# Sums of w_down: smaller transfers spread over the up stage, and half of the sums read back through the weights' buffers

## The chip, the core and the metric

The kernel runs on one core of a Trainium2 chip. The metric is the device time of one execution in microseconds, as the median of three runs. TensorE multiplies, ScalarE (ACT) and VectorE (DVE) prepare its operands, SyncE (SP) issues nearly all loads, and GpSimd (POOL) issues a few stores.

## The reference

It is one block of a hybrid transformer layer in float32 on 256 rows of width 2048: three attention branches, a gated merge and a projection, and behind them a gated feed-forward part. Only the latter bears on the change:

```
h2 = rms_norm(x, g_ffn)
u  = causal_depthwise_conv(h2 @ w_up, conv_w, conv_b)      # 2048 x 11264
u_gate, u_val = split(u, 2)
x  = x + (silu(u_gate) * u_val) @ w_down                   # 5632 x 2048
```

## The kernel before, in words

Every float32 weight is split into a high part (a rounded copy, made by ScalarE) and a low part (the rest, made by VectorE), and a product is formed from two or three matmuls with these parts. A weight tile therefore passes through four hands: a load into a buffer `raw`, a copy to `hi`, a subtraction to `lo`, and the matmuls. The pool `wp` has four buffers of each kind, of 4 KB in each of 128 partitions. A `raw` buffer is free for the next load when its low part is done; a `hi` or `lo` buffer is free when its last matmul has read it. SyncE works through its loads in one order, and each waits for its buffer, so a load that waits holds all that stand behind it.

The **up stage** (line 775 on) walks over w_up in 22 groups, one for each four feature tiles f0 and each half s of the columns (s = 0 the gate, s = 1 the value). A group has eight rounds over k. Each round loads one tile of 512 KB (line 142), splits it (143, 144) and issues 16 matmuls (791, 792). When a group is over, `conv` is queued for its two pairs of tiles, and its instructions (lines 726 to 748) run on ScalarE and VectorE beside the next group. After the value half, conv also multiplies gate and value and stores the result as `aT` (745 to 748), so the groups with s = 0 carry the longer conv.

The **down stage** uses one level of Strassen's scheme for a part of its work. An "eight" multiplies two tiles of k in the plain way: 8 products, 24 matmuls of 512 columns. A "seven" multiplies two tiles of k with 7 products, 21 matmuls; for it sums of w_down's blocks and sums of the activations are needed. The sums of the activations (`forms`, lines 818 to 836, result `sf`) are made by VectorE and ScalarE during the down stage. The sums of w_down are made already in the up stage by `weight_sums` (line 755): in each of the first 18 groups it loads two rows of tiles, 1 MB, into `r` (line 760), makes four additions on VectorE (764 to 768) and stores 1 MB to a tensor T in DRAM from GpSimd's queue (770). The pool `sp` holds two buffers `r`. In the down stage `seven` (line 884) loads two tiles of w_down, 256 KB and 512 KB, into `raw` buffers and the two halves of T, 512 KB each, called t13 and t42, into buffers `tt` of a pool `dn` (line 843). This pool has two buffers `tt` and lies on the memory of the convolution's pool, so it opens when the last convolution is over.

The two halves of the output's columns are done one after the other. The order of eights (e) and sevens (s) is written out in `PLANS` (line 40). A scheduler orders the instructions of each engine by what it takes to be ready, except for those that are kept in program order; the loads of `raw` tiles, the splits in the up stage and the additions on `r` keep to it as far as the code marks them. The stores to T are the only work of GpSimd's queue in this stage.

## Time and profile before

| what | value |
|---|---|
| median of three runs | 1524.01 us |
| the three runs | 1524.01, 1516.52, 1524.95 us |
| the profiled execution's own time | 1516.09 us |
| its span, first to last instruction | 1514.4 us |
| mean granted TensorE clock | 0.998 |
| up stage with sums | about 765 to 1180 us of the span |
| up stage without | 1180 to 1270 us |
| down stage | 1270 to 1508 us |
| TensorE busy | 1492.3 us, 99% of the span |

Times within the profile are microseconds from the span's start. In a timeline row stand the start, the duration, the engine, the line of the kernel, the operation with its output and inputs and, in brackets, how long the engine had stood idle and what ended that. Rows of waits give the engine and line that waited, what it waited for, the total, how often, and the longest. Rows of the chain of waits give start, duration and the work on the chain. Matmuls overlap each other in the trace, so the distance from one start to the next tells their pace, and not their duration.

### The profile page before, as it was taken

To read this page: it belongs to the slowest core of one execution; us is meant where nothing else is said; L and a number is where in the kernel's file an instruction comes from. 1 tells how busy PE (TensorE), PEld (TensorE's weight loads), DVE (VectorE), ACT (ScalarE), POOL (GpSimd) and SP (SyncE) were. 2 spreads that over 40 slices of the span, in tenths; PEclk is the share of its full clock that TensorE was granted. 3 is DMA by queue.
4 is the path that set the end of the run, shared out by engine and by line. 5 is a ranking of instruction groups with operands and counts; after the bars stand their busy time and mean duration, and the time that the engine had idled before them with its cause. 6 is when DMAs were issued, how large, how long until landed. Compare 5 with 4: busy or idle time off the path is not lost.

```text
span 1514.4 us, 20053 instructions
## 1 busy us (share of the span) xinstructions
PE 1492.3 (99%) x7411; PEld 1254.3 (83%) x7411; DVE 1021.5 (67%) x1291; ACT 856.8 (57%) x1211; POOL 25.8 (2%) x64
## 2 busy tenths in 40 slices
PE   9999999999999999999999999999999999899998
PEld 7888888888888888888888888888888888788876
DVE  5766566455655556565567778778778767877666
ACT  6755455368444444444566757657667766564553
POOL 0000000001000000000000000000000000000000
PEclk9999999999999999999999999999999999999999
DMA  8675475475666666665587787787877765787875
GB/s 299 202 205 155 130 219 154 127 215 154 194 200 208 191 205 194 192 193 184 182 264 267 248 296 255 271 282 257 294 279 249 223 196 171 263 280 258 262 271 176
DMA packets 151504, 335.55 MB, mean 222 GB/s; under 512 B 10714, under 2 KB 19566, under 8 KB 149102
## 3 DMA queue, kind: packets, MB, share of 16 engines
q1 hardware_dynamic: 147486, 313.29, 65.6%
q0 software_dynamic: 2592, 18.88, 3.0%
q10 hardware_dynamic: 1328, 2.11, 0.4%
q8 instruction: 58, 0.95, 0.3%
q14 instruction: 40, 0.33, 0.1%
HBM read 313.26 MB, written 20.97 MB: 221 GB/s over the span
## 4 chain that ended last, share of the span: by engine, by line
PE 74%; DMA 9%; DVE 9%; ACT 5%; issue 3%; POOL 0%; SPq 0%; DVEq 0%; ACTq 0%; POOLq 0%
PE u L791 9%; DMA raw_u<-in_w_up_dram 7%; PE g L154 5%; PE g L156 5%; PE g L155 5%; PE u L792 5%; PE d L859 4%; PE d L858 4%; PE d L857 4%; DVE lo_u L144 3%; PE s L154 2%; PE s L156 2%; PE f L154 2%; PE s L155 2%; PE f L155 2%
## 5 line engine op out<-in xcount | busy, mean ns | idle before, releaser
L791 PE MATMUL u<-hT,hi_u 128*128 128x512 f32 x1408 | 495.7, 397 | 0.1
L792 PE MATMUL u<-hT,lo_u 128*128 128x256 f32 x1408 | 396.0, 281 | 7.6 <-DVE lo_u L144 7.6
L791 PEld LDWEIGHTS u<-hT,hi_u 128*128 128x128 f32 x1408 | 264.3, 188 | 63.7 <-issue 0.5
L144 DVE TENSOR_TENSOR lo_u<-raw_u,hi_u 128x1024 fp32r<-128x1024 f32 x176 | 213.5, 1219 | 95.5 <-ACT hi_u L143 95.4
L792 PEld LDWEIGHTS u<-hT,lo_u 128*128 128x128 f32 x1408 | 265.9, 189 | 10.7 <-DVE lo_u L144 10.4
L143 ACT CAST hi_u<-raw_u 128x1024 fp32r<-128x1024 f32 x176 | 181.8, 1048 | 144.0 <-DMA raw_u<-in_w_up_dram 87.6
L144 DVE TENSOR_TENSOR lo_g<-raw_g,hi_g 128x1024 fp32r<-128x1024 f32 x96 | 117.6, 1228 | 101.4 <-ACT hi_g L143 98.8
L143 ACT CAST hi_g<-raw_g 128x1024 fp32r<-128x1024 f32 x96 | 100.8, 1052 | 121.7 <-PE g L155 97.5
L154 PE MATMUL g<-hi_g,xT 128*128 128x512 f32 x384 | 150.9, 393 | 0.0
L156 PE MATMUL g<-lo_g,xT 128*128 128x512 f32 x384 | 149.6, 390 | 0.0
L155 PE MATMUL g<-hi_g,xT 128*128 128x512 f32 x384 | 149.5, 389 | 0.0
L852 ACT CAST hi_d<-raw_d 128x1024 fp32r<-128x1024 f32 (+1 forms) x88 | 83.6, 963 | 42.5 <-PE d L858 29.6
L853 DVE TENSOR_TENSOR lo_d<-raw_d,hi_d 128x1024 fp32r<-128x1024 f32 (+1 forms) x88 | 95.1, 1110 | 15.0 <-ACT hi_d L852 15.0
L857 PE MATMUL d<-hi_d,aT 128*128 128x512 f32 x246 | 95.7, 389 | 0.0
L858 PE MATMUL d<-hi_d,aT 128*128 128x512 f32 x246 | 95.7, 389 | 0.0
L859 PE MATMUL d<-lo_d,aT 128*128 128x512 f32 x246 | 95.7, 389 | 0.0
L156 PEld LDWEIGHTS g<-lo_g,xT 128*128 128x128 f32 x384 | 72.1, 188 | 15.4
L155 PEld LDWEIGHTS g<-hi_g,xT 128*128 128x128 f32 x384 | 72.1, 188 | 14.5
L154 PEld LDWEIGHTS g<-hi_g,xT 128*128 128x128 f32 x384 | 72.1, 188 | 14.5
L738 ACT ACTIVATE z<-u,taps 128x256 f32<-128x256 f32 x176 | 74.6, 496 | 0.0
L739 DVE TENSOR_TENSOR y<-y,z 128x512 f32<-128x512 f32 x88 | 60.7, 690 | 19.1 <-ACT z L738 16.3
L853 DVE TENSOR_TENSOR lo_t<-tt,hi_t 128x1024 fp32r<-128x1024 f32 x36 | 44.1, 1225 | 39.8 <-ACT hi_t L852 39.7
(314 smaller groups left out, 2617.0 us busy)
## 6 DMA issues: line engine op xcount, KB each, us to landing
raw_u<-in_w_up_dram SPq DMA_DIRECT2D x176, 512.0 KB, 4.7
raw_g<-in_w_in_dram SPq DMA_DIRECT2D x96, 512.0 KB, 3.7
raw_d<-in_w_down_dram SPq DMA_DIRECT2D x70, 512.0 KB, 5.5
r<-in_w_down_dram SPq DMA_DIRECT2D x36, 512.0 KB, 7.3
T<-r POOLq DMA_DIRECT2D x18, 1024.0 KB, 7.7
tt<-T SPq DMA_DIRECT2D x36, 512.0 KB, 4.8
raw_f<-in_w_in_dram SPq DMA_DIRECT2D x32, 512.0 KB, 3.6
raw_s<-in_w_in_dram SPq DMA_DIRECT2D x32, 512.0 KB, 3.6
```

Source lines behind the costliest of these rows:

```text
L143: pin(nc.scalar.copy(hi[:, :m], raw[:, :m]))
L144: pin(nc.vector.tensor_tensor(lo[:, :m], raw[:, :m], hi[:, :m].bitcast(F32), ALU.subtract))
L154: nc.tensor.matmul(o, lhsT=xh, rhs=wh, start=first, stop=False)
L155: nc.tensor.matmul(o, lhsT=xl, rhs=wh, start=False, stop=False)
L156: nc.tensor.matmul(o, lhsT=xh, rhs=wl, start=False, stop=last)
L791: nc.tensor.matmul(ps, lhsT=hi[:, j, c], rhs=hT[:, k + j, :], start=first, stop=False)
L792: nc.tensor.matmul(ps[:, :S], lhsT=lo[:, j, c], rhs=hT[:, k + j, :S], start=False, stop=last)
L852: nc.scalar.copy(hi[:, :n], src)
L853: nc.vector.tensor_tensor(lo[:, :n], src, hi[:, :n].bitcast(F32), ALU.subtract)
L857: nc.tensor.matmul(o, lhsT=ah, rhs=w[0], start=first, stop=False)
L858: nc.tensor.matmul(o, lhsT=al, rhs=w[0], start=False, stop=False)
L859: nc.tensor.matmul(o, lhsT=ah, rhs=w[1], start=False, stop=last)
```

## The change

It has three parts.

1. `weight_sums` loads its 1 MB as four pieces of 256 KB, one behind each of a group's first four w_up tiles, where it loaded two of 512 KB behind the second. The first two additions move from the fifth round of the group to the sixth, the other two stay in the seventh. The store becomes two of 512 KB, which the code issues in the first and third round of the next group. A list `adding` with a count of rounds to wait keeps several of these alive.
2. `load_sums` takes a `raw` buffer for t42 of each seven, and also for t13 of the very first one. Only the other t13 use `tt`.
3. The order of the second half of the columns has its sevens one eight earlier: two eights ahead and three behind, where three stood ahead and two behind.

```diff
-PLANS = ("eee" + "se" * 8 + "eee", "eee" + "se" * 4 + "sse" * 3 + "ee")
+PLANS = ("eee" + "se" * 8 + "eee", "ee" + "se" * 4 + "sse" * 3 + "eee")
...
         r = sp.tile([P, 2, 2, 512], F32, tag="r", name=f"r_{nb}_{p}")
-        for j in range(2):
+        for j, n in ((0, 1), (0, 0), (1, 1), (1, 0)):
             tc.keep_in_program_order(
-                nc.sync.dma_start(r[:, j].rearrange("p a n -> p (a n)"), dv[:, 2 * p + j, n0 : n0 + PIECE])
+                nc.sync.dma_start(r[:, j, n], dv[:, 2 * p + j, n0 + n * 512 : n0 + (n + 1) * 512])
             )
-        yield
+            yield 1
+        yield 1
         b01 = r[:, 0, 1]
         tc.keep_in_program_order(nc.vector.tensor_tensor(r[:, 0, 0], r[:, 0, 0], b01, ALU.add))
         tc.keep_in_program_order(nc.vector.tensor_tensor(b01, b01, r[:, 1, 1], ALU.add))
-        yield
+        yield 1
         tc.keep_in_program_order(nc.vector.tensor_tensor(r[:, 1, 1], r[:, 1, 1], r[:, 0, 0], ALU.add))
         tc.keep_in_program_order(nc.vector.tensor_tensor(r[:, 1, 0], r[:, 1, 0], r[:, 1, 1], ALU.add))
         T = dram.tile([P, 2, 1024], F32, name=f"T_{nb}_{p}")
-        nc.gpsimd.dma_start(T, r.rearrange("p a b n -> p a (b n)"))
         made[nb, p] = T
-        yield
...
+        for h in range(2):
+            yield 2
+            nc.gpsimd.dma_start(T[:, h], r[:, h].rearrange("p b n -> p (b n)"))
+
+    adding = []
+
+    def add_on():
+        for a in list(adding):
+            if a[1] > 1:
+                a[1] -= 1
+                continue
+            try:
+                a[1] = next(a[0])
+            except StopIteration:
+                adding.remove(a)
...
-            adding = [weight_sums(*asked.pop(0))] if asked and f0 < HEAD else []
+            if asked and f0 < HEAD:
+                adding.append([weight_sums(*asked.pop(0)), 0])
...
-                if k in (2, 8, 12):
-                    for a in adding:
-                        next(a)
+                add_on()
+                if k == KT - 2 and f0 == HEAD - 4 and s == 1:
+                    while adding:
+                        add_on()
...
-    def load_sums(T, h, name):
-        t = down_pool().tile([P, PIECE], F32, tag="tt", name=f"tt{h}_{name}")
+    def load_sums(T, h, name, early):
+        if h or early:
+            t = wp.tile([P, PIECE], F32, tag="raw", name=f"raw_t{h}_{name}")
+        else:
+            t = down_pool().tile([P, PIECE], F32, tag="tt", name=f"tt{h}_{name}")
         nc.sync.dma_start(t, T[:, h])
...
-        t13, t42 = (load_sums(T, h, f"{n0}_{p}") for h in range(2))
+        t13, t42 = (load_sums(T, h, f"{n0}_{p}", n0 == 0 and p == 0) for h in range(2))
```

Three places of the built order show what moves. The first is SyncE's queue at the start of a group of the up stage (`raw_u` are tiles of w_up, `r` the blocks of w_down). Before, both halves stand behind the second tile:

```order
L142 DMA raw_u_0_0_7112<-in_w_up_dram 128x2x512
L142 DMA raw_u_0_2_7170<-in_w_up_dram 128x2x512
L760 DMA r_4_7192<-in_w_down_dram 128x1024 x2
L142 DMA raw_u_0_4_7195<-in_w_up_dram 128x2x512
L142 DMA raw_u_0_6_7217<-in_w_up_dram 128x2x512
L142 DMA raw_u_0_8_7239<-in_w_up_dram 128x2x512
```

With the change:

```order
L142 DMA raw_u_0_0_7122<-in_w_up_dram 128x2x512
L760 DMA r_4_7145<-in_w_down_dram 128x512
L142 DMA raw_u_0_2_7183<-in_w_up_dram 128x2x512
L760 DMA r_4_7145<-in_w_down_dram 128x512
L142 DMA raw_u_0_4_7206<-in_w_up_dram 128x2x512
L760 DMA r_4_7145<-in_w_down_dram 128x512
L142 DMA raw_u_0_6_7230<-in_w_up_dram 128x2x512
L760 DMA r_4_7145<-in_w_down_dram 128x512
L142 DMA raw_u_0_8_7253<-in_w_up_dram 128x2x512
```

Two pieces instead of two halves stand ahead of the third tile, and one more ahead of each of the next two.

The second is VectorE in the middle of a group with s = 0 (`lo_u` are low parts, `r` the additions, `y` and `aT` belong to conv). Before:

```order
L144 TENSOR_TENSOR lo_u_0_8_7683<-raw_u_0_8_7681,hi_u_0_8_7682 128x1024
L748 TENSOR_TENSOR aT_6213<-y_0_7361,aT_6213 128x2x256
L764 TENSOR_TENSOR r_6_7634<-r_6_7634 128x512
L739 TENSOR_TENSOR y_1_7598<-y_1_7598,z_10_1_7601 128x512
L765 TENSOR_TENSOR r_6_7634<-r_6_7634 128x512
L739 TENSOR_TENSOR y_1_7598<-y_1_7598,z_10_1_7605 128x512
L144 TENSOR_TENSOR lo_u_0_10_7707<-raw_u_0_10_7705,hi_u_0_10_7706 128x1024
L745 TENSOR_TENSOR y_0_7377<-y_0_7377,y_1_7598 128x512
L144 TENSOR_TENSOR lo_u_0_12_7729<-raw_u_0_12_7727,hi_u_0_12_7728 128x1024
```

With the change:

```order
L144 TENSOR_TENSOR lo_u_0_8_7703<-raw_u_0_8_7701,hi_u_0_8_7702 128x1024
L748 TENSOR_TENSOR aT_6213<-y_0_7377,aT_6213 128x2x256
L144 TENSOR_TENSOR lo_u_0_10_7725<-raw_u_0_10_7723,hi_u_0_10_7724 128x1024
L739 TENSOR_TENSOR y_1_7617<-y_1_7617,z_10_1_7620 128x512
L765 TENSOR_TENSOR r_6_7593<-r_6_7593 128x512
L739 TENSOR_TENSOR y_1_7617<-y_1_7617,z_10_1_7624 128x512
L766 TENSOR_TENSOR r_6_7593<-r_6_7593 128x512
L745 TENSOR_TENSOR y_0_7393<-y_0_7393,y_1_7617 128x512
L144 TENSOR_TENSOR lo_u_0_12_7749<-raw_u_0_12_7747,hi_u_0_12_7748 128x1024
```

The low part of the sixth tile (`lo_u_0_10`) stands four operations earlier; the same operations stand ahead of the seventh (`lo_u_0_12`).

The third is VectorE ahead of the first seven (`fr` and `sf` are the forms of the activations, `lo_t` the low parts of the two sums). Before:

```order
L748 TENSOR_TENSOR aT_10208<-y_0_10891,aT_10208 128x2x256
L831 TENSOR_TENSOR fr_11175<-fd_11170 128x256
L832 SCALAR_TENSOR_TENSOR fr_11175<-fr_11175,rbc 128x128
L827 TENSOR_TENSOR fd_11309<-aT_6213 128x512
L833 TENSOR_TENSOR fr_11175<-fr_11175,rbc 128x128
L830 TENSOR_TENSOR rbc<-aT_6213 128x256
L836 TENSOR_TENSOR sf<-fr_11175,sf 128x4x128
```

With the change, where lines 846 to 851 are the forms:

```order
L748 TENSOR_TENSOR aT_10262<-y_0_10945,aT_10262 128x2x256
L871 TENSOR_TENSOR lo_t_0_0_11308<-raw_t_0_0_11286,hi_t_0_0_11307 128x1024
L846 TENSOR_TENSOR fr_11229<-fd_11224 128x256
L847 SCALAR_TENSOR_TENSOR fr_11229<-fr_11229,rbc 128x128
L842 TENSOR_TENSOR fd_11363<-aT_6213 128x512
L848 TENSOR_TENSOR fr_11229<-fr_11229,rbc 128x128
L871 TENSOR_TENSOR lo_t_0_0_11318<-raw_t_0_0_11288,hi_t_0_0_11317 128x1024
L851 TENSOR_TENSOR sf<-fr_11229,sf 128x4x128
```

Both low parts of the sums now stand ahead of the last instruction of the first form; before they stood behind two forms.

1 line of the change is left out of this document (removed).

## The prediction, made before the changed kernel was run

> **What bounds the kernel now.** I read the page first, then the idle times of TensorE, then windows of equal work, and only then the two places where TensorE stops.
>
> ```profile
> span 1514.4 us, 20053 instructions
> PE 1492.3 (99%) x7411; PEld 1254.3 (83%) x7411; DVE 1021.5 (67%) x1291; ACT 856.8 (57%) x1211; POOL 25.8 (2%) x64
> ...
> PE u L792 <- DVE lo_u L144: 7.6, 8, 1.2
> ```
>
> TensorE is busy for 99% of the span, and the change adds and removes no matmul. So all that can be won is the time in which TensorE stands or runs below its pace. In the up stage the waits row says it: 7.6 us in 8 stops, all for the low part of a weight tile, none over 1.2 us. The down stage is read from counts, since its matmuls all have 512 columns:
>
> ```profile
> core 0: us, PE busy (x) PEld busy (x) DVE busy (x) ACT busy (x) POOL busy (x), PEclk, DMA share, GB/s
> 1280.00:1300.00 20.00, 15.94 (x62) 12.00 (x61) 17.25 (x29) 9.25 (x13) 0.00 (x0) 0.91 0.61 196
> 1300.00:1380.00 80.00, 80.00 (x354) 66.24 (x354) 65.78 (x85) 47.62 (x52) 0.00 (x0) 1.00 0.87 289
> 1450.00:1500.00 50.00, 47.59 (x203) 37.21 (x202) 34.76 (x35) 27.91 (x30) 0.00 (x0) 1.00 0.74 253
> ```
>
> Undisturbed, 354 matmuls take 80 us: 0.226 us each, so a "seven" (21 matmuls) is 4.75 us and an "eight" (24) 5.42 us. From 1280 to 1300 there are 62 where that pace gives 88.5: 26.5 x 0.226 = 6.0 us lost around the first seven. From 1450 to 1500 there are 203 for 221: 18 x 0.226 = 4.1 us lost around the three places with two sevens in a row. So 7.6 + 6.0 + 4.1 = 17.7 us are to be had, 1.2% of the run, and no more.
>
> **Part 1: sums of w_down in the up stage.** Here is one group of eight rounds before a stop (queue of SyncE, GpSimd's store, and the chain):
>
> ```profile
> 891.52 0.93 SPq L760 DMA_DIRECT2D r<-in_w_down_dram  x2
> ...
> 918.93 0.93 SPq L760 DMA_DIRECT2D r<-in_w_down_dram  x2
> ...
> 896.66 0.53 POOL L770 DMA_DIRECT2D T<-r  x1 [20.70 <-DVE r L768]
> ...
> 897.26 1.05 ACT L143 CAST hi_u<-raw_u 128x1024 fp32r<-128x1024 f32 x1 [1.82 <-DMA raw_u<-in_w_up_dram]
> ...
> 894.05 10.05 DMA raw_u<-in_w_up_dram
> 904.20 1.06 ACT hi_u L143
> ...
> raw_u<-in_w_up_dram SPq DMA_DIRECT2D x176, 512.0 KB, 4.7
> raw_d<-in_w_down_dram SPq DMA_DIRECT2D x70, 512.0 KB, 5.5
> r<-in_w_down_dram SPq DMA_DIRECT2D x36, 512.0 KB, 7.3
> raw_d<-in_w_down_dram SPq DMA_DIRECT2D x18, 256.0 KB, 5.4
> ```
>
> The third w_up tile of the group stands behind 1 MB of w_down in its queue and shares the engines with the 1 MB store that starts 2.6 us later: it lands after 10.05 us where the median is 4.7. The wait then travels through VectorE:
>
> ```profile
> 913.01 1.22 DVE L144 TENSOR_TENSOR lo_u<-raw_u,hi_u 128x1024 fp32r<-128x1024 f32 x1
> 914.14 0.68 DVE L748 TENSOR_TENSOR aT<-y,aT 128x512 fp32r<-128x512 f32 x1
> 914.75 0.68 DVE L764 TENSOR_TENSOR r<-r 128x512 f32<-128x512 f32 x1
> ...
> 917.22 1.22 DVE L144 TENSOR_TENSOR lo_u<-raw_u,hi_u 128x1024 fp32r<-128x1024 f32 x1
> ...
> 914.28 0.38 PE L792 MATMUL u<-hT,lo_u 128*128 128x256 f32 x1 [1.11 <-DVE lo_u L144]
> 918.49 0.39 PE L792 MATMUL u<-hT,lo_u 128*128 128x256 f32 x1 [1.16 <-DVE lo_u L144]
> ```
>
> TensorE stops twice in this group, for the fifth low part (914.28) and for the sixth (918.49). Two things change. In the queue only 512 KB instead of 1 MB of w_down stand ahead of the third tile: at the 289 GB/s of the long window 512 KB are 1.8 us, so it should land after about 8.2 us, and the fifth part with it, against a stop of 1.11. On VectorE the first two additions and the y rows around them now stand behind the sixth low part, not ahead of it: it moves up by four operations, 917.22 - 914.75 = 2.5 us, against a stop of 1.16; for this kind either change is enough. The low part after it keeps the same operations ahead of it. The second w_up tile gets 256 KB ahead, 0.9 us by the same rate; it is read at 897.26, 6.9 us before the third where one round (22.7 us a group, eight rounds) is 2.8, so it has 4.1 us more to give.
>
> New issues: 36 more on SyncE and 18 more on GpSimd. SyncE's cost 0.93 us per two (the row at 891.52), 18 groups x 0.93 = 17 us spread over 415 us in a queue that mostly waits for VectorE; GpSimd stands idle for 20.70 us before the store. Both are hidden. A new wait: a group's first quarter waits for both stores of two groups before, and the w_up tiles queue behind it. The store issued at 896.66 would have landed at 906.7 even in the 10.05 us of the slow tile; its buffer is asked for at 918.93 now, and one round earlier with the change, which leaves 9 us. Without that cover every microsecond would be one of w_up. The store's spread is not what it seems: it waits for VectorE's additions alone, so each half starts when its additions end, about a round apart. Bounds for the part: nothing won (0) and all won (-7.6). I take **-7.1**, near the full end, since each kind of stop is covered by more than its length.
>
> On this the Trainium skill speaks against the change: DMA: Bandwidth & Descriptors, section Rules for kernel authors, asks for at least 1 MiB per DMA, and its section on the anatomy of a DMA puts a fixed cost of about 2 us on each. By that, 54 more transfers are some 108 us of fixed cost, an estimate from that page of the Trainium skill: 1614 us if all of it lay on the path, the sum below if none did. Here a 256 KB load lands after 5.4 us and a 512 KB one after 5.5, which bears out a large fixed part; what it cannot show is whether that part is paid in the queue or beside other transfers. The rival "the pieces cost as much as wholes" below takes this up from rows.
>
> **Part 2: first seven.** Now its two sums wait for a pool that opens only when the last convolution is over:
>
> ```profile
> 1277.30 1.22 DVE L853 TENSOR_TENSOR lo_d<-raw_d,hi_d 128x1024 fp32r<-128x1024 f32 x1
> 1279.37 1.22 DVE L853 TENSOR_TENSOR lo_d<-raw_d,hi_d 128x1024 fp32r<-128x1024 f32 x1
> 1285.85 0.42 DVE L831 TENSOR_TENSOR fr<-fd 128x256 f32<-128x256 f32 x1
> 1287.12 0.28 DVE L833 TENSOR_TENSOR fr<-fr,rbc 128x128 f32<-128x128 f32 x1
> 1288.09 0.69 DVE L836 TENSOR_TENSOR sf<-fr,sf 128x512 fp32r<-128x512 f32 x1 [0.23 <-ACT sf L835]
> ...
> 1285.74 6.26 DMA tt<-T
> ...
> 1288.32 0.40 PE L857 MATMUL d<-hi_d,sf 128*128 128x512 f32 x1
> 1288.84 0.49 PE L858 MATMUL d<-hi_d,sf 128*128 128x512 f32 x1
> 1293.20 0.53 PE L857 MATMUL d<-hi_t,sf 128*128 128x512 f32 x1 [3.63 <-ACT hi_t L852]
> 1295.05 0.63 PE L857 MATMUL d<-hi_t,sf 128*128 128x512 f32 x1
> ```
>
> TensorE stands until 1293.20 and then runs at 0.63 us a matmul for a while. With the change both sums go into w_down's own buffers, whose slots come free at 1278.5 and 1280.6 (the first two rows), so they land by 1284 and 1286 at 5.5 us. Then something else is late. VectorE now has the first sum's low part ahead of the forms (from 1285.85) and the second's ahead of the last form instruction: 1285.85 + 1.13 (as from 913.01 to 914.14) = 1287.0; from the start of L831 to the end of L833 are 1287.12 + 0.28 - 1285.85 = 1.55, 1288.55; another 1.13 gives 1289.7; the form ends 0.69 later, 1290.4. TensorE wanted it at 1288.55, one matmul after 1288.32. So about 1.8 us of the 6.0 stay: **-4.2**. Bounds: -6.0, and 0 if the second sum lands as late as the first does now.
>
> **Part 3: two sevens in a row.** The sums have two buffers, so a second seven's loads start when the first one's low parts are done:
>
> ```profile
> 1449.35 1.24 DVE lo_t L853
> 1450.60 5.54 DMA tt<-T
> 1456.24 1.05 ACT hi_t L852
> 1457.32 1.24 DVE lo_t L853
> ...
> 1464.67 6.82 DMA tt<-T
> ...
> 1394.47 0.68 DVE L954 TENSOR_TENSOR o<-xres,d 128x512 f32<-128x512 f32 x1
> 1404.75 1.05 ACT L852 CAST hi_t<-tt 128x1024 fp32r<-128x1024 f32 x1 [1.67 <-PE d L858]
> ```
>
> From one low part's end to the next are 1458.56 - 1450.59 = 8.0 us for 4.75 us of matmuls, less the lead of one seven's pieces. Now one sum of a seven is asked for two sevens ahead, and the other takes one of the four w_down slots, three of which each seven then uses. The chain that is late next ends at the eight behind the pair: its first tile waits for the slot of the first seven's second sum. Counted from the start of that seven: low part done at 2.2 (the high and low slots come free with the eight before), landed 7.8 (5.54), high 8.9, low 10.1; TensorE wants high at 9.5 and low at 9.95. That is 0.15 us late; with 6.82 it is 1.4. I take 0.5 at each of three places: 4.1 - 1.5, **-2.6**, bounds -4.1 and 0. In single sevens the same slot goes to the next seven's second w_down tile: landed at 7.8, high at 8.8, wanted at 4.75 + 5.42 + 0.68 = 10.85. That slack of 2.1 us means that the twelve single sevens cost nothing unless loads pass 7.6 us. The other order of the second half starts its sevens one eight earlier. They need the banks that the four output additions of the first half free; the last of these ends at 1395.2, and the first sum is now cast at 1404.75, so 1399.3 after the move. Cost nothing, with 4 us of cover.
>
> **Sum.** The profiled execution took 1516.1 us: 1516.1 - 7.1 - 4.2 - 2.6 = 1502.2. The runs shown (1516.52, 1524.01, 1524.95) and it have a mean of 1520.4, 4.3 above the profiled one, and no row says what the slower ones spend; the change gives no reason for it to go. So 1502.2 + 4.3 = 1506.5, **1506 us**, 1.2% below the median of 1524.01.
>
> **Rivals.**
> *The up stage keeps half of its stops* (12%): the same 4 MB pass in the same eleven microseconds, and the store's halves meet the quarters. For it: the late tile's window. Against: the VectorE order. -3 instead of -7.1: 1510.
> *The forms hold the first seven* (11%): if the second sum lands late, the low part on VectorE holds the form, TensorE stands as long as before. Part 2 gives 0: 1510.5. For it: 6.26 us for the same load; against: it starts 5 us earlier.
> *The pieces cost as much as wholes* (5%, slower): a 256 KB piece holds the queue as long as 512 KB (5.4 against 5.5 us to land). Then the third tile has as much ahead as now and the fourth 1 MB more, 3.6 us at 289 GB/s. The nine groups in which VectorE also multiplies two convolutions are those without slack: 9 x 3.6 = +32, parts 2 and 3 stay: 1516.1 + 32 - 6.8 + 4.3 = 1546. Against: loads of 512 KB follow each other at 289 GB/s with 5.5 us each, so most of a landing is not queue time.
> *Four slots are too few* (8%, slower): five tiles of a seven and an eight now share four slots. It decides from 7.6 us per load (5.5 + 2.1 slack); at 9.5, near the row of 10.05, 15 pairs lose 1.9 each: +28, less 11.3 for parts 1 and 2: 1537. For it: the engines are at 0.87 from 1300 to 1380. Against: 5.5 is the median there, and the bytes are the same.
> *The change does not do what it says*: for the store that is so, as said, and costs nothing; for the loads the queue order shows it done.
>
> **How the numbers follow.** My forecast has 62%, with 2% for what I did not think of. Low end: all 17.7 us won and no run above the profiled one, 1498. High end: the milder rivals with the slowest run's excess (8.9), 1517; the two slower ones stay outside. What a measurement can tell from no change is about 0.5%, 7.6 us: 1516.4. The forecast and most of the two milder rivals lie below: 0.62 x 0.97 + 0.23 x 0.8 = 0.78 faster; 0.14 within; 0.08 slower, from the last two.
>
> **What would show it.** Part 1: waits of the up matmuls for the low part under 1 us in all, and the third w_up tile of a group landing in about 8 us. Part 2: the wait for the sum's high part at the first seven gone, one of 1 to 2 us for the form in its place, and no matmul of 0.63 us. Part 3: no wait for the sums in the second half, and short ones for a w_down tile behind each pair of sevens. I am wrong if the waits of the up stage stay, or if single sevens begin to wait for w_down tiles.

## Result

| | us |
|---|---|
| before, median of 10 runs | 1520.25 (1516.52 to 1524.95) |
| changed, median of 10 runs | 1512.46 (1507.57 to 1514.22) |
| ratio, 95% interval | 0.9941 (0.9925 to 0.9958) |
| profiled execution, before and changed | 1516.09 and 1511.22 |
| its span, before and changed | 1514.4 and 1509.5 |

The change makes the kernel 0.6% faster. The forecast was 1506 us and faster, with a range of 1498 to 1517: the side is right and the time lies in the range, but of the 13.9 us that the sum promised the profiled executions show 4.9. The medians lie 7.8 us apart; the other 2.9 us are in runs without a trace, and nothing here says what they are. Two of the three parts came as forecast or better. The third should have won 2.6 us; it lost 8.4.

### The profile page after: what moved, and what is told of

It reads as the page before. It is cut to its first block, busy times and chain, and to the rows that moved or that the text cites. A ratio compares the mean times of both kernels' runs of the same rounds, so it can differ in the third digit from the quotient of the medians.

```text
span 1509.5 us, 20128 instructions
## 1 busy us (share of the span) xinstructions
PE 1492.9 (99%) x7411; PEld 1252.9 (83%) x7411; DVE 1022.7 (68%) x1291; ACT 861.0 (57%) x1211; POOL 35.5 (2%) x82
## 4 chain that ended last, share of the span: by engine, by line
PE 87%; DMA 5%; DVE 3%; ACT 2%; issue 1%; POOL 0%; SPq 0%; DVEq 0%; ACTq 0%; POOLq 0%
PE u L805 22%; PE u L806 11%; PE g L154 5%; PE g L156 5%; PE g L155 5%; DMA raw_d<-in_w_down_dram 3%; PE d L877 2%; PE s L154 2%; PE s L156 2%; PE f L155 2%; PE s L155 2%; PE f L154 2%; PE f L156 2%; PE d L876 2%; PE d L875 2%; PE b L154 2%
## 5 line engine op out<-in xcount | busy, mean ns | idle before, releaser
L805 PE MATMUL u<-hT,hi_u 128*128 128x512 f32 x1408 | 497.8, 399 | 0.1
L806 PE MATMUL u<-hT,lo_u 128*128 128x256 f32 x1408 | 395.4, 281 | 0.0
L805 PEld LDWEIGHTS u<-hT,hi_u 128*128 128x128 f32 x1408 | 264.5, 188 | 66.3 <-issue 0.5
L806 PEld LDWEIGHTS u<-hT,lo_u 128*128 128x128 f32 x1408 | 266.0, 189 | 0.0
L144 DVE TENSOR_TENSOR lo_s<-raw_s,hi_s 128x1024 fp32r<-128x1024 f32 (+1 forms) x40 | 44.7, 1118 | 37.2 <-ACT hi_s L143 37.1
```

The source lines that it names most:

```text
L144: pin(nc.vector.tensor_tensor(lo[:, :m], raw[:, :m], hi[:, :m].bitcast(F32), ALU.subtract))
L805: nc.tensor.matmul(ps, lhsT=hi[:, j, c], rhs=hT[:, k + j, :], start=first, stop=False)
L806: nc.tensor.matmul(ps[:, :S], lhsT=lo[:, j, c], rhs=hT[:, k + j, :S], start=False, stop=last)
```

## The profile after

The waits of TensorE in the changed kernel, without those at the start of the program (engine and line that waited, who was waited for, total us, times, longest us):

```profile
PE d L877 <- DVE lo_d L871: 2.3, 5, 0.5
PE d L875 <- ACT hi_d L870: 2.3, 3, 1.2
PE d L877 <- DVE lo_t L871: 1.7, 3, 0.9
...
PE d L875 <- ACT sf L850: 0.6, 1, 0.6
```

No row of the up stage (L805, L806) is left: its 7.6 us of stops are gone. The 3.63 us in front of the first seven have become 0.6 us for its form. In their place stand waits for the high and low parts of w_down tiles and of sums, eleven of them, none long. Windows of equal length say where. First the changed kernel, then the kernel before (from, to, length, then busy time and instructions of TensorE, of its weight loads, VectorE, ScalarE and GpSimd, granted clock, DMA share, GB/s):

```profile
765.00:1180.00 415.00, 415.00 (x2355) 360.17 (x2355) 329.19 (x404) 286.81 (x442) 19.28 (x36) 1.00 0.82 276
1270.00:1300.00 30.00, 29.38 (x129) 23.73 (x128) 28.59 (x46) 18.48 (x26) 0.00 (x0) 1.00 0.75 254
1300.00:1380.00 80.00, 77.82 (x337) 62.44 (x336) 61.55 (x76) 43.06 (x48) 0.00 (x0) 1.00 0.81 266
1300.00:1480.00 180.00, 173.65 (x743) 139.05 (x742) 127.40 (x145) 96.31 (x106) 0.00 (x0) 0.99 0.79 262
```

```profile
765.00:1180.00 415.00, 407.41 (x2313) 353.12 (x2312) 321.39 (x396) 275.39 (x430) 9.72 (x18) 1.00 0.78 270
1270.00:1300.00 30.00, 25.94 (x107) 20.28 (x106) 25.74 (x41) 18.72 (x29) 0.00 (x0) 0.94 0.51 165
1300.00:1480.00 180.00, 177.78 (x780) 145.67 (x780) 132.01 (x154) 100.28 (x108) 0.00 (x0) 1.00 0.82 273
```

Read the counts. In 415 us of the up stage there are 42 matmuls more, 42 x 415/2355 = 7.4 us won (the next stage starts 7.6 us earlier, as the rows under part 2 below show). Around the first seven there are 22 more, 22 x 0.226 = 5.0 us won. From 1300 to 1480, where an undisturbed TensorE does 180/0.226 = 796, the kernel before did 780 (3.7 us lost) and the changed one does 743 (12.1 us lost): 8.4 us given back. The sum is -4.0 against a measured -4.9. The windows stand at fixed times and so cut different work in the two kernels: from its first matmul to its last the down stage takes 237.6 us before and 240.1 changed, 2.5 more, where the two windows give 8.4 - 5.0 = 3.4. From 1300 to 1380, where the kernel before did not stop at all (354), 17 are missing, 3.8 us: these are single sevens, which the prediction had costed at nothing.

The waits of the down stage above add up to 6.9 us and the counts to 12.9 (0.8 from 1270 to 1300 and 12.1 behind), for three reasons that the timelines show. A bar of 0.39 us hides the first 0.16 of every stop, since the next matmul could have started 0.226 behind the last; the matmul behind a stop starts 0.33 later and not 0.226; and at one place the clock is lower (last section).

One of the single sevens, in the timeline of the changed kernel: TensorE at the first matmul of the seven and at its stop, then VectorE.

```profile
1311.05 0.39 PE L875 MATMUL d<-hi_d,aT 128*128 128x512 f32 x1
...
1315.57 0.50 PE L877 MATMUL d<-lo_t,sf 128*128 128x512 f32 x1 [0.48 <-DVE lo_t L871]
```

```profile
1312.97 0.68 DVE L842 TENSOR_TENSOR fd<-aT 128x512 f32<-128x512 f32 x1
...
1314.29 1.23 DVE L871 TENSOR_TENSOR lo_t<-raw_t,hi_t 128x1024 fp32r<-128x1024 f32 x1
```

And the chain of waits of the changed kernel from 1300 us, in order of time (start, length, what):

```profile
1305.52 7.58 DMA raw_t<-T
...
1313.20 1.06 ACT hi_t L870
...
1314.29 1.24 DVE lo_t L871
...
1315.54 4.70 DMA raw_d<-in_w_down_dram
...
1320.34 1.06 ACT hi_d L870
```

The tile is the second sum of the seven, now in one of the four weight slots. Its low part is done at 1315.52, 4.5 us after the seven's first matmul at 1311.05. The prediction had it done after 2.2, which is what it is in the single sevens of the kernel before (2.3 to 2.6); in those of the changed kernel behind the first seven it is 2.9 to 5.2. Only then is the slot free and the next w_down tile asked for, at 1315.54: the end of one low part starts the next load, and so on round the ring. That is how a ring that is too short looks in a chain of waits: landing, high, low, landing, high, low, with hardly a gap. ScalarE shows it from the other side. Its waits from 1300 to 1380 us, changed and before:

```profile
ACT hi_d L870 <- DMA raw_d<-in_w_down_dram: 25.8, 16, 5.1
```

```profile
ACT hi_t L852 <- PE d L858: 14.9, 10, 1.7
...
ACT hi_d L852 <- DMA raw_d<-in_w_down_dram: 3.4, 2, 3.2
```

Before, ScalarE waited for TensorE to give back the parts: the tiles were there early. Now it waits for tiles to land. One row more, the landing of w_down tiles on the changed kernel's page (KB each, median us; single loads in this stretch took up to 8.1):

```profile
raw_d<-in_w_down_dram SPq DMA_DIRECT2D x70, 512.0 KB, 5.3
```

The reason is arithmetic that the prediction did not do. A seven and an eight are 10.17 us of matmuls. Before, four tiles in that time went through four slots, 10.2 us for each slot's turn. Now it is five tiles, 4/5 x 10.17 = 8.1 us a turn. A turn takes 5.3 for the landing, 0.1 to the start of the cast, 1.06 for the high and 1.24 for the low part, 7.7 us, when VectorE is free at once and the load is a median one. Often it is not so: other low parts and the forms stand ahead, and the sum in the chain above took 7.58 us to land.

## Experiments

Three explanations for the new stops stood against each other: **the slots** (five tiles through four), **the forms** (VectorE, in order, has them ahead of low parts), and **SyncE's order** (a sum fetched two sevens ahead waits for its buffer at the head of the queue and holds the w_down tile behind it). "Lost" below is (796 - matmuls from 1300 to 1480) x 0.226 us. Ratios are to runs of the kernel before that were taken beside each run; their medians were 1515.4 to 1516.2 us, so times are not to be compared with the 1520.25 above. Where no ratio is given, the kernel ran once, and its trace is what counts.

### The two halves apart

The up stage alone: weight_sums and its stepping as changed, plan, pools and loads of the down stage as before.

```diff
-PLANS = ("eee" + "se" * 8 + "eee", "ee" + "se" * 4 + "sse" * 3 + "eee")
+PLANS = ("eee" + "se" * 8 + "eee", "eee" + "se" * 4 + "sse" * 3 + "ee")
...
-    def load_sums(T, h, name, early):
-        if h or early:
-            t = wp.tile([P, PIECE], F32, tag="raw", name=f"raw_t{h}_{name}")
-        else:
-            t = down_pool().tile([P, PIECE], F32, tag="tt", name=f"tt{h}_{name}")
+    def load_sums(T, h, name):
+        t = down_pool().tile([P, PIECE], F32, tag="tt", name=f"tt{h}_{name}")
...
-        t13, t42 = (load_sums(T, h, f"{n0}_{p}", n0 == 0 and p == 0) for h in range(2))
+        t13, t42 = (load_sums(T, h, f"{n0}_{p}") for h in range(2))
```

> The up stage of the change alone (loads in four, stores in two, additions behind the sixth low part); the down stage and its plan as before. All times are of the profiled execution (before 1516.1, changed 1511.2). Theory: the up stage's gain is whole and does not depend on the down stage: its 7.6 us of stops go, nothing comes in the down stage, where 6.0 us at the first seven and 4.1 us at the pairs of sevens stay: 1516.1 - 7.6 = about 1508, ratio 0.995. So this part alone would be faster than the whole change by about 3 us. Rival, that the later and smaller stores of the sums delay something in the down stage: some of the stops of the single sevens (1300 to 1445 us) appear here too, and the time is 1511 or more.

Measured: ratio to before 0.9962 (0.9950 to 0.9975), profiled execution 1512.15. Its windows:

```profile
765.00:1180.00 415.00, 414.85 (x2353) 359.73 (x2352) 329.17 (x405) 286.79 (x440) 19.28 (x36) 1.00 0.81 277
1270.00:1300.00 30.00, 26.22 (x101) 20.32 (x100) 24.89 (x40) 16.15 (x23) 0.00 (x0) 0.89 0.62 202
1300.00:1480.00 180.00, 177.29 (x778) 145.50 (x778) 131.02 (x152) 99.49 (x108) 0.00 (x0) 1.00 0.81 270
```

The gain of the up stage is whole (2353 against 2355), and no single seven stops (the 18 missing matmuls are the pairs of sevens). The rival's cause falls: none of its stops came. Its time came all the same, 1512 where it said 1511 or more, 4 us above the theory. Part of that is the stop at the first seven: 32 matmuls of 133 are missing here, 7.2 us, where 26 were before, 5.9, with a granted clock of 0.89 for 0.94. The four other executions took 1508.9 to 1510.1.

The down stage alone is the complement: weight_sums as before, plan and load_sums as changed. A part of the edit, against the changed kernel:

```diff
-        for j, n in ((0, 1), (0, 0), (1, 1), (1, 0)):
+        for j in range(2):
             tc.keep_in_program_order(
-                nc.sync.dma_start(r[:, j, n], dv[:, 2 * p + j, n0 + n * 512 : n0 + (n + 1) * 512])
+                nc.sync.dma_start(r[:, j].rearrange("p a n -> p (a n)"), dv[:, 2 * p + j, n0 : n0 + PIECE])
             )
...
-                add_on()
-                if k == KT - 2 and f0 == HEAD - 4 and s == 1:
-                    while adding:
-                        add_on()
+                if k in (2, 8, 12):
+                    for a in adding:
+                        next(a)
```

> The down stage of the change alone (half of the sums through the weights' slots, the first seven's both halves there, the plan of the second half moved by one eight); the up stage as before. Theory: the down part is a loss by itself. It wins about 5 us at the first seven and gives some 8 us back at single sevens and at the pairs: 1516.1 + 2 to 3 = 1518.5, ratio 1.001 to 1.002, with stops at single sevens as in the changed kernel. Rival, that the stops at single sevens come from the new up stage: none here, and 1516.1 - 5 - 2 = 1509.

Measured: ratio 1.0011 (0.9998 to 1.0025), profiled 1514.82. Its windows:

```profile
1270.00:1300.00 30.00, 29.39 (x129) 23.80 (x128) 27.72 (x44) 21.66 (x32) 0.00 (x0) 1.00 0.67 227
1300.00:1480.00 180.00, 173.78 (x746) 138.16 (x745) 128.24 (x150) 95.18 (x104) 0.00 (x0) 1.00 0.78 262
```

The down part wins 5.0 us at the first seven and loses 11.4 - 3.7 = 7.7 us behind it. In that execution the unchanged up stage stopped for 5.7 us and not 7.6, so single executions differ by some 2 us there; this is a part of why its time is not above before. By the ratio the down part is worth nothing: what the change wins is its up part. Since the two were timed against other runs of the kernel before than the whole change, whether the whole is ahead of its up part alone is not settled.

### How many slots

Only the first seven's sums in the weight slots; four tiles through four again:

```diff
-        if h or early:
+        if early:
```

> The changed kernel, except that only the first seven takes its sums through the weights' slots; all the others use the two buffers of their own, as before. Theory, four slots for five tiles of a seven and an eight (a lap of landing 5.3 + high 1.06 + low 1.24 = 7.6 us, with whatever VectorE has ahead, against 4/5 of 10.17 = 8.1 us of matmuls): with four tiles again the lap has 10.2 us, so the stops of single sevens from 1300 to 1445 go, those of the pairs (about 4 us) are as before the change: 1516.1 - 7.6 - 5.2 = about 1503, ratio 0.992 or less. Rival, forms on VectorE: they stand at the same places here, so the stops of single sevens in the first half (about 4 us) stay: 1507. Rival, that prefetched sums ahead of w_down tiles in SyncE's queue are the cause: the built order has none of them here, so it expects what the theory of the slots expects.

Measured: ratio 0.9933 (0.9921 to 0.9944), profiled 1504.86. Its windows:

```profile
1300.00:1380.00 80.00, 80.00 (x355) 66.24 (x354) 62.07 (x77) 45.18 (x49) 0.00 (x0) 1.00 0.83 281
1300.00:1480.00 180.00, 176.56 (x772) 143.93 (x771) 131.87 (x150) 100.19 (x109) 0.00 (x0) 1.00 0.80 272
```

Not one stop from 1300 to 1380, with the forms on VectorE as they were. The forms alone are not the cause. The pairs of sevens lose 5.4 us, somewhat more than before, and the ratio is a little above the 0.992 expected.

All six slots in turn, for every tile from the first seven on, so that it does not matter which of them a tile gets:

```diff
+    ring = [-6]
+
+    def slot(name):
+        i = ring[0]
+        ring[0] += 1
+        if i < 0 or i % 6 < 4:
+            return wp.tile([P, PIECE], F32, tag="raw", name=name)
+        return down_pool().tile([P, PIECE], F32, tag="tt", name=name)
+
     def load(k, n0, n=PIECE):
-        raw = wp.tile([P, PIECE], F32, tag="raw", name=f"raw_d{n0}_{k}")
+        raw = slot(f"raw_d{n0}_{k}")
...
-        if h or early:
-            t = wp.tile([P, PIECE], F32, tag="raw", name=f"raw_t{h}_{name}")
-        else:
-            t = down_pool().tile([P, PIECE], F32, tag="tt", name=f"tt{h}_{name}")
+        t = slot(f"raw_t{h}_{name}")
```

> The changed kernel with all six slots (four of the weights, two of the sums) taken in turn by every tile of the down stage from the first seven on, so that six tiles of a seven and an eight go through six slots. Theory of the slots: the lap has 10.2 us for single sevens and about 7 us inside a pair of sevens with the eights' lead behind it, so stops go in single sevens and are under 2 us in all at the pairs: 1516.1 - 7.6 - 5.2 - 2 to 4 = 1499 to 1501, ratio 0.989. Rival, forms on VectorE: about 4 us stay in the first half's single sevens: 1504. Rival, SyncE's order: the loads stand in the order of use here, so it expects what the slots expect.

Measured: ratio 0.9889 (0.9876 to 0.9902), median 1499.18, profiled 1498.51. A window and, behind it, what ScalarE waited for from 1300 to 1480:

```profile
1300.00:1480.00 180.00, 180.00 (x796) 149.05 (x795) 137.46 (x157) 103.14 (x111) 0.00 (x0) 1.00 0.82 277
```

```profile
ACT hi_t L876 <- PE d L882: 34.6, 29, 1.7
...
ACT hi_d L876 <- DMA raw_d<-in_w_down_dram: 5.2, 5, 1.7
```

796 matmuls in 180 us: TensorE does not stop once, the pairs of sevens included. ScalarE waits for TensorE again and not for landings. The bytes, the additions, the forms and the plan are those of the change; the same 24 KB of slots per partition are handed out in another way, and with that the loads also stand in another order in SyncE's queue, which is tried by itself below. This kernel is faster than both: 1.1% below before.

A fifth slot alone, to see whether it is the number that counts. The five tiles take the four slots and one of the sums' two in turn, and the first sum of each seven keeps the other (the rest of `slot` as above):

```diff
+        if i < 0 or i % 5 < 4:
+            return wp.tile([P, PIECE], F32, tag="raw", name=name)
+        return down_pool().tile([P, PIECE], F32, tag="fifth", bufs=1, name=name)
...
-        raw = wp.tile([P, PIECE], F32, tag="raw", name=f"raw_d{n0}_{k}")
+        raw = slot(f"raw_d{n0}_{k}")
...
         if h or early:
-            t = wp.tile([P, PIECE], F32, tag="raw", name=f"raw_t{h}_{name}")
+            t = slot(f"raw_t{h}_{name}")
         else:
-            t = down_pool().tile([P, PIECE], F32, tag="tt", name=f"tt{h}_{name}")
+            t = down_pool().tile([P, PIECE], F32, tag="tt", bufs=1, name=f"tt{h}_{name}")
```

> The changed kernel with a fifth slot, taken from the sums' own two: the five tiles of a seven and an eight that go through the weights' slots take five slots in turn, and the first sum of every seven after the first has one slot of its own. Theory of the slots: single sevens have a lap of 10.2 us for 7.7 and do not stop from 1300 to 1430 (354 matmuls in 80 us); inside a pair of sevens the one slot has a lap of 7.8 us for 4.75, which costs up to 3 us at each of three pairs, less the lead of a seven's pieces: 3 to 8 us lost from 1430 to 1490. Rival, that the stops come with the partition of the tiles or the sums' order in the queue, not with the number of slots: 3 us or more lost from 1300 to 1380 as in the changed kernel.

Measured: profiled 1503.81. Its windows:

```profile
1300.00:1380.00 80.00, 80.00 (x354) 66.27 (x353) 63.56 (x79) 44.73 (x49) 0.00 (x0) 1.00 0.83 280
1300.00:1480.00 180.00, 178.15 (x782) 146.16 (x781) 134.61 (x154) 101.87 (x111) 0.00 (x0) 1.00 0.82 276
```

The same partition of the tiles as in the change, and one slot more: 354 for 337 from 1300 to 1380. What is lost, 3.2 us, lies at the pairs (2.8 from 1430 to 1490, 253 matmuls for 265.5, just under the 3 to 8 expected). The single slot of the first sums is short there: ScalarE waits 8.0 us in that stretch for their landing.

### The other two explanations

The loads of the down stage issued in the order of their use, slots as changed:

```diff
-        nc.sync.dma_start(raw[:, :n], dv[:, k, n0 : n0 + n])
+        tc.keep_in_program_order(nc.sync.dma_start(raw[:, :n], dv[:, k, n0 : n0 + n]))
...
-        nc.sync.dma_start(t, T[:, h])
+        tc.keep_in_program_order(nc.sync.dma_start(t, T[:, h]))
```

> The changed kernel with the same slots, but the loads of the down stage issued on SyncE in the order of their use, so that no sum's load stands ahead of a w_down tile of an earlier seven. Theory of the slots (five tiles through four): the lap is as long as before, so the stops between 1290 and 1445 us (4.6 us in gaps of over 0.4 us) and those at the pairs stay within 1 us: about 1511 in the profiled execution, ratio to before 0.994 to 0.997. Rival, SyncE's order (a prefetched sum waits for its buffer at the head of the queue and holds the w_down tile behind it): the stops of single sevens go as they did with six slots in turn and with only the first seven's sums in the weights' slots: 1506 to 1507, ratio 0.991.

Measured: ratio 0.9989 (0.9973 to 1.0005), profiled 1516.49. A window, and the longest wait of TensorE:

```profile
1300.00:1480.00 180.00, 174.27 (x755) 140.48 (x754) 129.79 (x145) 97.99 (x105) 0.00 (x0) 1.00 0.79 268
```

```profile
PE d L875 <- ACT hi_d L870: 4.9, 1, 4.9
```

Where the stops are, 9.3 us are lost for 12.1: most of them stay, though not within the 1 us expected, and the order of SyncE is at most the smaller part. The time of the whole is worse for a reason that the expectation did not have: with the fixed order the convolution's last operations and the first forms stand ahead of a w_down tile near 1274 us, and TensorE waits 4.9 us once for its high part. The stop lies outside the window. It cost more than its length: from 1270 to 1300 TensorE does 93 matmuls for 133, 9.0 us, at a granted clock of 0.89.

The forms shortened, slots as changed; five of six VectorE operations of the second to the eighth form left out, so that this kernel does not compute the reference's result:

```diff
+        if 1 <= p < 8:
+            q = flat[:, :512].rearrange("p (f q) -> p f q", f=4)
+            to = form_of(p)
+            nc.scalar.copy(to[:, :, 0], q)
+            nc.vector.tensor_tensor(to[:, :, 1], q, to[:, :, 0].bitcast(F32), ALU.subtract)
+            return
         nc.vector.tensor_tensor(
             d, two, v[:, 0, :, 1].unsqueeze(1).to_broadcast([P, 2, 2, P]), ALU.subtract
         )
```

> The changed kernel with five of the forms' six operations on VectorE left out for the second to eighth seven (their forms are copied from the convolution's rows as they are, so the output is not the reference's); of 2.8 us of VectorE a form, 0.7 stay. The slots are as changed: five tiles through four. Looked at from 1300 to 1380 us, where the change loses 17 matmuls, 3.8 us. Theory of the slots with VectorE's work as a part of the lap (7.7 us against 8.1, and up to 2.8 of forms ahead of a low part): without most of the forms the lap fits nearly always, and 1 us or less is lost. Rival, that the slots alone are short, as the second half shows, which has the same stops with few forms: 2.5 to 4 us stay.

Measured: profiled 1508.91. A window, and ScalarE's wait from 1300 to 1380:

```profile
1300.00:1380.00 80.00, 79.34 (x347) 64.37 (x346) 53.97 (x53) 42.42 (x45) 0.00 (x0) 1.00 0.82 271
```

```profile
ACT hi_d L876 <- DMA raw_d<-in_w_down_dram: 34.0, 20, 4.7
```

7 matmuls are missing for 17: 1.6 us for 3.8, between the two expectations. So both are in it: the ring is short without the forms too (ScalarE still waits 34 us for landings), and the forms in front of low parts on VectorE are the larger part of what is lost here. From 1380 to 1480, where only two forms are made in either kernel, this one does 407 matmuls and the changed one 408, of 442: there the ring stops TensorE without the forms. With a fifth or sixth slot the forms cost nothing from 1300 to 1380.

### The plan

Six slots, with the plan of the second half as it was before the change:

```diff
-PLANS = ("eee" + "se" * 8 + "eee", "ee" + "se" * 4 + "sse" * 3 + "eee")
+PLANS = ("eee" + "se" * 8 + "eee", "eee" + "se" * 4 + "sse" * 3 + "ee")
```

> The kernel with six slots in turn (1496.8 us span, no stop between 1300 and 1490 us), with the plan of the second half put back as it was before the change (three eights first, two last). Theory: the plan matters only through the slots, so with no stop left it costs and wins nothing: ratio to before within 0.1% of that kernel's 0.989. Rival, the moved eight is itself worth something, since the last pair of sevens then stands further from the end: stops of 1 us or more come back near 1485, ratio 0.990 or more.

Measured: ratio 0.9894 (0.9878 to 0.9910) against 0.9889, and 795 matmuls from 1300 to 1480. The moved eight is worth nothing once the ring is long enough.

### The up stage taken apart

Four kernels, each the changed one but for one or two things in weight_sums, looked at from 765 to 1180 us (stops of 7.6 us before, none changed). The stops are of the two kinds of the prediction. Before, three of the eight come at a group's fifth tile, 2.0 us, and five at its sixth, 5.6 us. One whole store right after the additions:

```diff
-        for h in range(2):
-            yield 2
-            nc.gpsimd.dma_start(T[:, h], r[:, h].rearrange("p b n -> p (b n)"))
+        nc.gpsimd.dma_start(T, r.rearrange("p a b n -> p a (b n)"))
```

> The changed kernel, except that each sum is stored in one transfer of 1 MB right after its additions, as before; loads in four and the order on VectorE as changed. Up stage alone (765 to 1180 us). Theory, the store's size costs nothing once only 512 KB of w_down stand ahead of the third w_up tile: under 1 us of stops. Rival, the store was half of what made that tile late: 2 to 4 us of stops come back.

```profile
765.00:1180.00 415.00, 415.00 (x2355) 360.01 (x2354) 329.02 (x404) 288.08 (x441) 9.71 (x18) 1.00 0.80 276
```

No stop, 2355 matmuls: the store in halves wins nothing. The additions at their old places, loads in four:

```diff
             yield 1
-        yield 1
         b01 = r[:, 0, 1]
...
-        yield 1
+        yield 2
         tc.keep_in_program_order(nc.vector.tensor_tensor(r[:, 1, 1], r[:, 1, 1], r[:, 0, 0], ALU.add))
```

> The changed kernel, except that the additions stand at their old places on VectorE (the first two ahead of the sixth low part); loads in four and stores in two as changed. Up stage alone (765 to 1180 us). By the prediction's working the loads in four are enough for both kinds of stop: under 1 us stays. Rival, VectorE's order was the cause of the second kind or of both: 3 to 7 us stay.

```profile
PE u L805 <- DVE lo_u L144: 2.6, 4, 1.0
```

2.6 us stay, between the two expectations, and all four stops are of the second kind, at a group's sixth tile: the loads in four end the first kind and about half of the second. Whole loads, additions and store as changed:

```diff
-        for j, n in ((0, 1), (0, 0), (1, 1), (1, 0)):
+        yield 1
+        for j in range(2):
             tc.keep_in_program_order(
-                nc.sync.dma_start(r[:, j, n], dv[:, 2 * p + j, n0 + n * 512 : n0 + (n + 1) * 512])
+                nc.sync.dma_start(r[:, j].rearrange("p a n -> p (a n)"), dv[:, 2 * p + j, n0 : n0 + PIECE])
             )
-            yield 1
-        yield 1
+        yield 4
```

> The changed kernel, except that w_down's sums are loaded in two transfers of 512 KB right behind each other as before; the additions stay at their new place behind the sixth low part, the store in halves. Looked at in the up stage alone (765 to 1180 us, 7.6 us of stops before, none in the changed kernel). By the prediction's working the order on VectorE ends only the second stop of a group (sixth low part), and the late third w_up tile, the first stop, is the queue's: about half, 3 to 4 us, stay. Rival, VectorE's order was the whole cause: under 1 us stays.

```profile
PE u L806 <- DVE lo_u L144: 17.1, 18, 1.6
```

Neither expectation held: 18 stops, 17.1 us, and 1535.64 us in all. The same with one whole store on top (the two edits above together):

> The changed kernel with whole loads of w_down's sums and one whole store, so that of the up stage's change only the place of the additions on VectorE is left. Up stage alone (765 to 1180 us; stops of 7.6 us before, 17.1 with whole loads, new additions and the store in halves). Theory, the later additions move the store onto the next group's loads, and a first half that leaves 1.6 us behind these loads is what hurts most: with one whole store, later still, 4 to 9 us. Rival, the later additions alone are what hurts, whatever the store's size: 14 to 20 us.

```profile
PE u L804 <- DVE lo_u L144: 1.6, 1, 1.6
```

One stop of 1.6 us, less than the 4 to 9 expected; the rival, that later additions hurt by themselves, falls. The stop is of the first kind, at a fifth tile whose group's third was cast 10.1 us behind its issue. So either half of the edit ends most of the stops, the additions' new place with whole loads (1.6 us stay) or the loads in four with the old places (2.6 stay); which of the two is better these single executions can't tell, since the same up stage differed by 2 us above. Both together end all in the changed kernel, and left up to 0.9 us in other executions of the same up stage (the trace of six slots with the old plan).

Stops are not all that counts here. With one stop this kernel does more matmuls in the window than the changed one with none (2355):

```profile
765.00:1180.00 415.00, 413.37 (x2373) 362.15 (x2373) 329.78 (x408) 285.83 (x448) 9.73 (x18) 1.00 0.79 277
```

A group without a stop takes 22.6 us throughout the changed kernel and 22.2 in most of this one; the kernel before has groups of both kinds. No run shows why, and no part of the change was meant for it. The store in halves is neutral beside loads in four (with a whole store TensorE does not stop either) and costs 15.5 us beside whole loads. In that kernel GpSimd issues the first half, in most groups, 1.6 to 2.2 us behind the whole loads, and the whole store comes 5.7 to 6.9 us behind them; that the bytes then meet the third w_up tile was not shown; the runs show only that the pair is bad.

## Why the prediction was right, and where not

**What bounds the kernel**: right. The stops were there to be won, 17.7 us by the prediction; the kernel with six slots has none left from 1300 to 1480, and its span is 17.6 us shorter (1514.4 to 1496.8). That they were all and "no more" is not so: with the old plan the span is 1494.3, 20.1 us shorter. The 2.5 us between the two lie in the up stage, 495.7 us from first matmul to last for 498.5, where groups take 22.2 us as well as 22.6; the prediction took the pace between stops to be one.

**Part 1, -7.1**: right, 7.4 measured. The w_up tiles come earlier, as the working had it: the third tile of a group is cast at most 8.2 us behind its issue in the groups with sums, where two groups had 9.8 and 10.2 before (8.2 was the working's landing). What ScalarE waited for them from 765 to 1180 us, before and changed:

```profile
ACT hi_u L143 <- DMA raw_u<-in_w_up_dram: 87.6, 36, 5.9
```

```profile
ACT hi_u L143 <- DMA raw_u<-in_w_up_dram: 28.3, 16, 3.9
```

The two kinds of stop have the causes that the working gave them: in one execution each, the loads in four alone leave none of the first kind, and the additions alone none of the second but 1.6 of the first kind's 2.0 us. "For this kind either change is enough" was too much: the loads in four alone leave 2.6 of the second kind's 5.6 us. That the store's spread costs nothing is right for this change. On the rule of the Trainium skill, DMA: Bandwidth & Descriptors, section Rules for kernel authors, that a DMA should have at least 1 MiB for maximum bandwidth: the 54 more and smaller transfers cost nothing that shows, no stop being left, but the kernel with whole transfers and later additions stops for only 1.6 us, so the runs do not speak against the rule either.

**Part 2, -4.2**: too small, 5.0 measured. The first matmul of the down stage, before and changed:

```profile
1270.60 0.40 PE L857 MATMUL d<-hi_d,aT 128*128 128x512 f32 x1
```

```profile
1262.97 0.40 PE L875 MATMUL d<-hi_d,aT 128*128 128x512 f32 x1
```

The whole stage is 7.6 us earlier, by part 1, and times of the two kernels compare with this shift. SyncE's queue where the two sums of the first seven are asked for, the end of the first form, and TensorE:

```profile
1270.91 2.43 SPq L863 DMA_DIRECT2D raw_t<-T  x2
...
1281.96 0.69 DVE L851 TENSOR_TENSOR sf<-fr,sf 128x512 fp32r<-128x512 f32 x1
...
1281.90 0.50 PE L875 MATMUL d<-hi_d,sf 128*128 128x512 f32 x1 [0.62 <-ACT sf L850]
...
1282.94 0.39 PE L876 MATMUL d<-hi_d,sf 128*128 128x512 f32 x1
```

The sums are asked for at 1270.91 + 7.63 = 1278.5 on the time scale of before, as read from the slots, and the form ends at 1282.65 + 7.63 = 1290.3 where the working had 1290.4. Both are right. What was wrong is who waits for the form's end: TensorE stops only for its high part, made by ScalarE, 0.6 us. In the built order two matmuls of the second sum now stand ahead of the stop and three others behind it, so the first that reads the form's low part comes at 1282.94 and does not wait; the working had it one matmul behind the first that reads the form, and 1.8 us late. The clock stays at 1.00 (the window from 1270). The prediction's "0.63 us a matmul" is the length of a bar; the starts in those rows of before are 0.43 us apart.

**Part 3, -2.6**: wrong, +8.4 us from 1300 to 1480. The step that failed reads "that slack of 2.1 us means that the twelve single sevens cost nothing unless loads pass 7.6 us". Loads did not pass 7.6 in the median (5.3; two of eighteen recorded landings of w_down tiles from 1300 to 1480 did, with 7.9 and 8.1), and the single sevens stopped. The working followed one tile from one seven to the next and took its low part to be done 2.2 us into its seven, as if the tile were always there in time. In the seven shown it measured 4.5. The bound is not the slack of one tile but the turn of the ring: four slots for five tiles give 8.1 us, of which a tile needs 7.7 when nothing stands ahead of it, and a fifth slot alone ended the stops of the single sevens. The row that would have told it was in the profile of before, as the median landing of 5.5 us, beside the two parts' 1.05 and 1.24.

**Rivals.** "Four slots are too few" named the place and the mechanism, and had both numbers wrong: it decided at a median of 5.3 us a load and not from 7.6, and it cost 8.4 us and not 28. It may be that every stop gives the ring the time that it lacks and so keeps the loss small; no run tests that. The condition of "the pieces cost as much as wholes" came and its price did not: a piece of 256 KB lands after 7.3 us on the changed kernel's page, as a whole of 512 KB did before, and yet the third tile is not late. "The forms hold the first seven" and "the up stage keeps half of its stops" did not come.

**The total.** By the windows the sum was short by the 11.0 us of part 3, and 1.1 us came back from parts 1 and 2; the 0.9 us that this leaves open are the windows' edges. The forecast of 1506 had added 4.3 us for runs above the profiled one; the changed kernel's median is 1.2 us above its own. That the measured 1512 still lies in the range is luck as far as the sum goes: it is owed to the range. The range's high end, 1517, is itself some 2 us above what either of the milder rivals gives by its own terms (1516.1 - 3 - 4.2 - 2.6 + 8.9 = 1515.2 and 1516.1 - 7.1 - 2.6 + 8.9 = 1515.3).

## What to carry to other kernels

Count a ring of buffers by its turn: slots divided by tiles in a period, times the period, must be longer than landing plus all that reads the slot, with what stands ahead on engines that work in order; the slack of one tile followed by hand does not show it. When tiles of several kinds pass through one stage, hand out all slots in turn rather than a fixed few to each kind: here the same six slots lost 12.1 us with five tiles through four of them, 3.2 with five tiles through five, and nothing with all in turn. When a background transfer makes a critical one late, look both at its place in the queue and at its work on the engine behind, and take the edit apart before crediting a piece of it: here either of the two was nearly enough, and the split store was worth nothing.

## What the hardware did unasked

At one place two stops in a row went with a lower clock although neither was long. At the second pair of sevens, timeline of TensorE in the changed kernel:

```profile
1464.07 0.50 PE L875 MATMUL d<-hi_d,aT 128*128 128x512 f32 x1 [1.17 <-ACT hi_d L870]
...
1465.33 0.50 PE L877 MATMUL d<-lo_d,aT 128*128 128x512 f32 x1 [0.52 <-DVE lo_d L871]
...
1466.30 0.63 PE L877 MATMUL d<-lo_d,aT 128*128 128x512 f32 x1
...
1469.29 0.42 PE L875 MATMUL d<-hi_d,aT 128*128 128x512 f32 x1
```

```profile
1462.00:1470.00 8.00, 6.31 (x19) 4.38 (x19) 4.22 (x4) 4.56 (x5) 0.00 (x0) 0.79 0.84 302
```

After waits of 1.17 and 0.52 us the seven matmuls from 1466.30 to 1469.29 start 0.43 us apart where 0.226 is the pace: 1.4 us beside the stops, and a granted clock of 0.79 from 1462 to 1470. Two shorter stops did not do it: at the pairs of sevens of before, waits of 0.53 and 0.53 us within 1.3 us, and of 0.64 and 0.53, left the pace at 0.226. In the up stage of before, waits of up to 1.2 us left the clock at 1.00. The Trainium skill, TensorE: Matmul & The Clock Gate, Part 1, has the clock halve after an idle window of about 3.4 us. The pace of 0.43 agrees with a halved clock; no wait here was half as long as that window, so the trace does not agree that one must be idle throughout.
